# The low part of a filter network's last weights, on 128 stacked rows instead of 64

## The chip, the cores and the metric

The kernel runs on one core of one Trainium2 chip. The time is device time in microseconds, from the first to the last instruction of the program. TensorE is called PE in the profile, its weight loads PEld, VectorE is DVE, ScalarE is ACT, GpSimd is POOL and SyncE, which issues most DMAs, is SP.

## What is computed

One inference step of a two-layer backbone, for a prompt of 128 positions and a sample of 512. Each layer normalises its input, multiplies it with `w_in`, runs three mixers side by side (retention, Hyena, a gated linear recurrence), and multiplies the result with `w_out`. The Hyena mixer convolves along the sequence with long filters, and these filters come from a small network over the position. That network is what the change touches:

```python
hid = jnp.sin(fr[0] * (z @ w1 + b1))            # z (L, 33), w1 (33, 64)
hid = jnp.sin(fr[1] * (hid @ w2 + b2))          # (L, 64)
h = (hid @ w3).reshape(L, 2, 2, 512)            # w3 (64, 2048)
h = h * jnp.exp(-t * deltas)[:, None, None, :]
h = h / (jnp.sum(jnp.abs(h), axis=0, keepdims=True) + EPS)
```

It runs for both lengths, L = 128 and L = 512, in each of the two layers; the kernel keeps both lengths side by side, 640 columns.

## The kernel before

**Split products.** The operands of large products are kept in two parts, a high part in a rounded format (`fp32r`) and a low part, the rest. A product is then the sum of high x high, high x low and low x high.

**The last layer of the filter network.** The 64 hidden values of a position are stacked on 128 partitions: rows 0 to 63 of `hstk` hold the high part, rows 64 to 127 the low part. `w3` (64 rows) is loaded twice, on partitions 0 to 63 and on 64 to 127 (`load_w3`, L598). One product of `w3h`, the high part of the weights on all 128 rows, with `hstk` gives high x high + high x low. `w3l`, the low part of the weights, lies on 64 partitions and is multiplied with the upper 64 rows of `hstk`, which gives low x high. Both go to the same PSUM tile.

**Taps, in `filters` (L594).** Each layer's filters are made in four units `u` of two halves `t`. For one (u, t), `taps(u, t)` converts 256 columns of weights (ACT at L619, DVE at L620), then does four pairs of products (L630 and L631: two directions d by two halves n of 320 columns), each pair into a PSUM tile `hg`. DVE multiplies each tile with a window into SBUF (L632), ACT sums absolute values (L634), and DVE scales and combines (L636 to L647). Later the taps are transposed on PE (`turn`, tiles `ft` and `ftp`), folded (`fold`, L507, on DVE and POOL), split into parts (`blocks`, L534) and transformed by a DFT as products with constant matrices (`dft`, tiles `spr`, `spi`, `spa`).

**Order.** PE runs its instructions in the order in which they are emitted. Threads are generators that emit one stage and yield an estimated time; `pump` chooses the next ready one. A product counts its columns for this clock:

```python
n = x.free_size()
return queue(T.matmul(out, lhs, x, start=start, stop=stop), w * n / 2400 * (4 if x.dtype == F32 else 1))
```

The filters of layer 0 run as a thread among the norm, the modulation (`ada_gen`, tiles `ada`, weights `aw`) and the input projection of layer 0 (tiles `z`, `mtile_steps`). The filters of layer 1 run among the output projection of layer 0 (tiles `o`, `out_proj`) and the modulation of layer 1. The small PSUM tiles (`pat`) share four buffers in turn: `ft`, `ftp`, `hg`, `spr`, `spi`, `spa` and others take the next one, and wait until its last reader is done. The projections use two larger buffers of their own (`pmt`).

Of the kernel before, what the change touches and what calls it, by code (L numbers as in the profile page):

```python
# [16 lines left out]
P = 128  # L17
# [189 lines left out]
# which engine, and at which step: bit masks and step numbers  # L207
# [5 lines left out]
# lead times of the threads, in units of TensorE work  # L213
# [9 lines left out]
def step_kernel(ctx: ExitStack, tc: tile.TileContext, xT, ada_w, w_in, w_out, vecs, fw1, fw2, fw3, lgw, sret,  # L223
# [16 lines left out]
    def f(ap):  # L240
        return ap.bitcast(F32)
# [4 lines left out]
    hstk, w3h, w3l = R1[:, 0:640], R1[:, 640:896], R1[0:64, 896:1152]  # L246
# [61 lines left out]
    # ---------------------------------------------------------------- order of the work on TensorE  # L308
    # TensorE runs its instructions in the order of emission. Threads are generators that emit one
    # stage and yield the time (us of TensorE work) until the next one's operands are there.  # L310
# [49 lines left out]
    def gap(us):  # L360
        """other threads' work while the operands of the next instruction come."""
        end = clk[0] + us
        pump()
        while clk[0] < end:
            clk[0] = min([end] + [max(t.ready, clk[0]) for t in ths])
            pump()
# [9 lines left out]
    # ---------------------------------------------------------------- setup  # L376
# [10 lines left out]
    # decay rates: softplus(-x) of the LRU lambdas and the retention logits  # L387
# [6 lines left out]
    def decays():  # L394
        x, sp = ar(spx_, 32), ar(sp_, 32)
        E = G if XG else V
        for l in range(DEPTH):
            E.tensor_copy(ar(spx_ + 16 * l, 8), vec(l, "lam", 0, 8))
            E.tensor_copy(ar(spx_ + 16 * l + 8, 8), vec(l, "rl", 0, 8))
        a, n, y, q = ar(tA_, 32), ar(tB_, 32), ar(tC_, 32), ar(tD_, 32)  # L400

        def fma(out, u, c, w, op0, op1):
            """(u op0 c) op1 w"""
            if XG:
                G.tensor_scalar(out, u, c, None, op0=op0)
                G.tensor_tensor(out, out, w, op=op1)
            else:
                V.scalar_tensor_tensor(out, u, c, w, op0=op0, op1=op1)

        V.scalar_tensor_tensor(a, x, -1.0, x, op0=ALU.mult, op1=ALU.max)  # L410
        E.tensor_scalar(a, a, 85.0, None, op0=ALU.min)
        E.tensor_scalar(n, a, 1.0 / math.log(2.0), MAGIC, op0=ALU.mult, op1=ALU.add)
        E.tensor_scalar(n, n, MAGIC, None, op0=ALU.subtract)
        fma(y, n, LN2_1, a, ALU.mult, ALU.subtract)
        fma(q, n, LN2_2, y, ALU.mult, ALU.add)
        E.tensor_copy(y, q)
        # 2^-n by its exponent
        E.tensor_scalar(a.bitcast(mybir.dt.int32), n, -float(2 ** 23), 127.0 * 2 ** 23, op0=ALU.mult, op1=ALU.add)
        E.tensor_scalar(q, y, 1.0 / 5040, None, op0=ALU.mult)
        for c in (720, 120, 24, 6, 2, 1):  # L420
            fma(q, q, 1.0 / c, y, ALU.add, ALU.mult)
        fma(q, q, 1.0, a, ALU.add, ALU.mult)
        E.tensor_scalar(a, q, 2.0, None, op0=ALU.add)
        V.reciprocal(a, a)
        E.tensor_tensor(a, a, q, op=ALU.mult)
        E.tensor_tensor(y, a, a, op=ALU.mult)
        E.tensor_scalar(q, y, 1.0 / 15, None, op0=ALU.mult)
        for c in (13, 11, 9, 7, 5, 3):
            fma(q, q, 1.0 / c, y, ALU.add, ALU.mult)
        fma(q, q, 1.0, a, ALU.add, ALU.mult)  # L430
        E.tensor_scalar(a, x, -1.0, 0.0, op0=ALU.mult, op1=ALU.max)
        fma(sp, q, 2.0, a, ALU.mult, ALU.add)
        E.tensor_scalar(ar(sp2_, 32), sp, 2.0, None, op0=ALU.mult)
        E.tensor_scalar(ar(spm4_, 32), sp, -4.0, None, op0=ALU.mult)
        # retention columns: half rate and minus rate
        for l in range(DEPTH):
            E.tensor_scalar(ar(sp2_ + 16 * l + 8, 8), ar(sp_ + 16 * l + 8, 8), 0.5, None, op0=ALU.mult)
            E.tensor_scalar(ar(spm4_ + 16 * l + 8, 8), ar(sp_ + 16 * l + 8, 8), -1.0, None, op0=ALU.mult)
        for i in range(DEPTH):
            E.tensor_scalar(ar(hgb_[i], 16), vec(i, "lgb", 0, 16), 0.5, None, op0=ALU.mult)  # L440

    # ---------------------------------------------------------------- adaLN
# [10 lines left out]
    def ada_gen(l, r, early=False):  # L453
        """Third r of the modulation of layer l; two weight slots per yield."""
# [41 lines left out]
    # ---------------------------------------------------------------- hyena filters  # L496
# [10 lines left out]
    def fold(src, off, eng):  # L507
        """src [P, 4, 256] time blocks -> the eight folded blocks: four at off, four in place."""
        f = ar(off, 1024).rearrange("p (b c) -> p b c", b=4)
        eng.tensor_tensor(f[:, 0:2], src[:, 0:2], src[:, 2:4], op=ALU.add)  # L510
        eng.tensor_tensor(f[:, 2:4], src[:, 0:2], src[:, 2:4], op=ALU.subtract)
        V.scalar_tensor_tensor(src[:, 1], f[:, 3], SQH, src[:, 0], op0=ALU.mult, op1=ALU.add)
        V.scalar_tensor_tensor(src[:, 3], f[:, 1], SQH, src[:, 2], op0=ALU.mult, op1=ALU.add)
        V.scalar_tensor_tensor(src[:, 0], f[:, 3], -SQH, src[:, 0], op0=ALU.mult, op1=ALU.add)
        V.scalar_tensor_tensor(src[:, 2], f[:, 1], SQH, src[:, 2], op0=ALU.mult, op1=ALU.subtract)
        V.tensor_tensor(f[:, 0], f[:, 0], f[:, 1], op=ALU.add)
        V.scalar_tensor_tensor(f[:, 1], f[:, 1], -2.0, f[:, 0], op0=ALU.mult, op1=ALU.add)
        return f[:, 0:2], f[:, 2:4], src[:, 1:4:2], src[:, 0:3:2]
# [4 lines left out]
    def cf0(ri, i):  # L523
        """class 0: half the columns for block i, zeros for the other block's"""
        return cf(192 * ri + 64 * i)

    def mm3(out, w, x, first=True, last=True):
        """out += w.T x of operands split in two parts."""
# [5 lines left out]
    def blocks(fo, pr, cls, eng):  # L534
        """the one or two folded blocks of class cls (E0, prompt, E2, O1, O3), split: [(high, low), ...]"""
# [9 lines left out]
    def dft(out, bl, cls, ri):  # L545
        """part ri of class cls of its blocks."""
# [16 lines left out]
    def hidden(l):  # L563
        """the hidden layers of the layer's filter network, split and stacked."""
# [29 lines left out]
    def filters(l):  # L594
        """Spectra of the layer's filters, to DRAM; yields between pieces of work."""
# [16 lines left out]
        def taps(u, t):  # L612
# [7 lines left out]
            V.tensor_tensor(w3l.rearrange("p (d c) -> p d c", d=2), w3[0:64], f(w3h[0:64]).rearrange("p (d c) -> p d c", d=2),  # L620
# [3 lines left out]
            for d in range(2):  # L624
                h = ar(ROPE_ if d and t else fb_ + 640 * d, 640)
                fd.append(h)
                for n in range(2):
# [3 lines left out]
                    mm(out, w3l[:, 128 * d:128 * d + 128], hs[0:64], start=False, stop=True)  # L631
# [21 lines left out]
        def turn(u, i, t):  # L653
            """part i (sum, difference) of taps t of unit u, time-major."""
# [14 lines left out]
        def hook(u, c):  # L669
            """what goes with class step c (sums 0 to 4, differences 5 to 9) of unit u"""  # L670
# [64 lines left out]
    # ---------------------------------------------------------------- norm  # L735
# [5 lines left out]
    def sumsq(acc, k, hf=None):  # L741
        """squares of X_k: added to acc, but for the last ones (taken by halves), which stay in their buffer."""
# [10 lines left out]
    def rstd(nm, n, *srcs):  # L753
        """1/rms of n columns of summed squares, on all partitions."""
# [15 lines left out]
    def make_h0():  # L770
        """h of layer 0 from the normalised x."""
# [29 lines left out]
    def make_h(l, hf, ks, rs):  # L801
        """columns of half hf of h's tiles ks, from x and 1/rms"""
# [18 lines left out]
    # ---------------------------------------------------------------- projections  # L821
# [16 lines left out]
    def mtile_steps(ps, h, lo, ns):  # L838
        """h @ w of one tile into the halves ns, four products per step."""
# [28 lines left out]
    def both(l, *mts):  # L868
        """two tiles side by side, while the operands come one by one"""
# [15 lines left out]
    def first_half(l, mt):  # L885
        """the half 0 of a tile, before the other's operands are there"""
# [17 lines left out]
    def to_time(src, nm):  # L904
        """five transposes of a channel-major [P, 644]: the sample's four blocks and the prompt's."""
# [6 lines left out]
    # ---------------------------------------------------------------- hyena  # L912
# [164 lines left out]
    def conv_consts():  # L1077
        """the inverse transform's matrices, split: high at 2048, low at 4096 and (the prompt's) in hstk."""
# [10 lines left out]
    # ---------------------------------------------------------------- retention  # L1089
# [4 lines left out]
    def ret_tables(l, early):  # L1094
        """decay tables; the early ones go to DRAM until their place is free."""
# [76 lines left out]
    def ret_in(l, h, start):  # L1172
        """q, k and v of a head"""
# [83 lines left out]
    # ---------------------------------------------------------------- RG-LRU  # L1257
# [11 lines left out]
    def lru_pad_init(l):  # L1269
        """per (ct, dir) the four pad columns of the scan input: zero, and the initial state next to the sample."""  # L1270
# [78 lines left out]
    # ---------------------------------------------------------------- gates, output projection  # L1349
# [104 lines left out]
    # ---------------------------------------------------------------- schedule  # L1454
# [243 lines left out]
```

## Time and profile before

| | |
|---|---|
| median of 3 runs | 1324.87 us (1324.29 to 1326.26) |
| span of the profiled execution | 1326.2 us |
| PE busy | 1184.6 us, 89% |
| PE weight loads busy | 1104.7 us, 83% |
| DVE busy | 910.2 us, 69% |
| ACT busy | 619.0 us, 47% |
| POOL busy | 629.9 us, 48% |
| instructions | 20592 |
| mean granted clock of PE | 0.954 |

Busy time is the time in which an engine has an instruction under way. A wait is shown with what ended it: the engine, the tile and the line whose result came last; "issue" stands for a wait that nothing in the profile explains. The end of a matmul is modelled, so the starts of weight loads and matmuls tell more than the durations. The granted clock is 1.00 at 2.4 GHz and 0.50 at 1.2 GHz.

### The profile page before, as it was taken

How to read it: one execution, taken by the hardware profiler on the slowest of the kernel's cores; microseconds unless marked ns; L12 is line 12 of the kernel's file. 1: busy time of each engine (PE TensorE's matmuls, PEld its weight loads, DVE VectorE, ACT ScalarE, POOL GpSimd, SP SyncE). 2: the span in 40 equal slices, each digit the busy share in tenths (PEclk: the TensorE clock that was granted, in tenths of full speed). 3: DMA queues.
4: the chain of work that ended last, by engine and by line, in shares of the span. 5: the costliest groups of instructions: out<-in, count | busy, mean ns of one | idle time of the engine just before them, and what ended most of it. 6: DMA issues, size and time to landing. Idle time of an engine off the chain costs nothing. (4 is left out here: it accounts for less than half of the span.)

```text
span 1326.2 us, 20592 instructions
## 1 busy us (share of the span) xinstructions
PE 1184.6 (89%) x7944; PEld 1104.7 (83%) x7944; DVE 910.2 (69%) x1412; ACT 619.0 (47%) x1099; POOL 629.9 (48%) x529
## 2 busy tenths in 40 slices
PE   4688899998989889869999988899999989889996
PEld 2476779997989889857777778899998989888996
DVE  6888886685865777666887669665477576676313
ACT  3557555343334566644455554432443366555220
POOL 2644436554555644442334438454354654545431
PEclk9798899999999899988999989899999998999998
DMA  9632323312211112244454623122221211124222
GB/s 331 212 126 90 120 87 111 130 62 72 88 39 62 56 48 65 90 130 134 151 165 154 213 70 114 50 102 80 73 88 41 68 48 64 34 69 122 69 63 80
DMA packets 52114, 131.62 MB, mean 99 GB/s; under 512 B 6230, under 2 KB 14182, under 8 KB 50736
## 3 DMA queue, kind: packets, MB, share of 16 engines
q1 hardware_dynamic: 51668, 130.21, 29.5%
q8 instruction: 62, 1.02, 0.3%
q14 instruction: 36, 0.29, 0.1%
q10 hardware_dynamic: 348, 0.11, 0.0%
HBM read 112.38 MB, written 17.92 MB: 98 GB/s over the span
## 5 line engine op out<-in xcount | busy, mean ns | idle before, releaser
L296 ACT ACTIVATE r<-arena 128x512 fp32r<-128x512 f32 (+1 forms) x72 | 43.6, 607 | 113.8 <-PE u L328 37.7
L296 ACT ACTIVATE arena<-arena 128x644 f32<-128x644 f32 (+5 forms) x84 | 63.5, 772 | 46.3 <-DVE arena L1392 33.8
L296 ACT ACTIVATE rt<-arena 128x512 fp32r<-128x512 f32 (+1 forms) x42 | 29.1, 692 | 98.9 <-POOL arena L980 78.8
L328 PE MATMUL u<-r,cfwd 128*128 128x256 f32 x432 | 63.2, 295 | 12.4 <-ACT r L296 9.6
L328 PEld LDWEIGHTS u<-r,cfwd 128*128 128x128 f32 x432 | 58.4, 201 | 14.5 <-ACT r L296 10.8
L328 PE MATMUL hg<-r 128*128 128x320 f32 (+1 forms) x128 | 48.6, 441 | 18.9 <-DVE r L589 9.5
L542 POOL TENSOR_TENSOR r<-arena,r 128x512 fp32r<-128x512 f32 (+1 forms) x24 | 31.7, 1322 | 68.1 <-ACT r L296 58.0
L1392 DVE SCALAR_TENSOR_TENSOR arena<-o,arena 128x128 f32<-128x128 f32 (+2 forms) x48 | 18.5, 432 | 60.2 <-PE o L328 60.1
L328 PEld LDWEIGHTS hg<-r 128*128 128x128 f32 (+1 forms) x128 | 25.7, 201 | 40.9 <-issue 18.7
L980 POOL TENSOR_TENSOR arena<-arena 128x256 f32<-128x256 f32 x40 | 39.2, 980 | 34.4 <-DVE arena L976 17.7
L975 DVE TENSOR_TENSOR arena<-u,arena 128x512 f32<-128x512 f32 x40 | 27.5, 688 | 31.7 <-PE u L328 31.7
L296 ACT ACTIVATE arena<-z 128x644 f32<-128x644 f32 x44 | 31.0, 705 | 35.9 <-PE z L328 35.8
L328 PE MATMUL spr<-r,cfwd 128*128 128x256 f32 x192 | 36.8, 303 | 10.6 <-ACT rt L296 4.0
L328 PEld LDWEIGHTS spr<-r,cfwd 128*128 128x128 f32 x192 | 29.0, 198 | 17.2 <-ACT rt L296 5.5
L983 POOL TENSOR_TENSOR rt<-arena,rt 128x512 fp32r<-128x512 f32 x24 | 31.9, 1331 | 20.0 <-ACT rt L296 20.0
L542 DVE TENSOR_TENSOR r<-arena,r 128x512 fp32r<-128x512 f32 x32 | 34.2, 1067 | 9.6 <-ACT r L296 8.6
L296 ACT ACTIVATE r<-rt 128x512 fp32r<-128x512 f32 (+3 forms) x50 | 28.2, 564 | 21.0 <-PE spi L328 7.7
L328 PE MATMUL spi<-r,cfwd 128*128 128x256 f32 x168 | 35.7, 301 | 0.9 <-DVE rt L632 0.9
L542 POOL TENSOR_TENSOR r<-rt,r 128x256 fp32r<-128x256 f32 (+1 forms) x16 | 19.2, 1199 | 36.4 <-ACT r L296 36.3
L296 ACT ACT_TABLE_LOAD x27 | 34.6, 1283 | 3.8 <-DMA arena<-in_vecs 3.3
L542 POOL TENSOR_TENSOR dm<-rt,r 128x256 fp32r<-128x256 f32 (+1 forms) x16 | 21.6, 1347 | 28.6 <-ACT r L296 28.6
L1334 DVE TENSOR_TENSOR_SCAN lr<-arena 128x644 f32<-128x644 f32 x8 | 18.4, 2294 | 24.1 <-POOL arena L1329 24.1
(1285 smaller groups left out, 4279.2 us busy)
## 6 DMA issues: line engine op xcount, KB each, us to landing
w<-in_w_in SPq DMA_DIRECT2D x80, 512.0 KB
aw<-in_ada_w SPq DMA_DIRECT2D x96, 256.0 KB
wo<-in_w_out SPq DMA_DIRECT2D x32, 384.0 KB
spec<-arena SPq DMA_DIRECT2D x16, 640.0 KB
arena<-spec SPq DMA_DIRECT2D x8, 1280.0 KB
arena<-in_xT SPq DMA_DIRECT2D x16, 320.0 KB
rt<-in_c_win SPq DMA_DIRECT2D x4, 640.0 KB
arena<-xspill SPq DMA_DIRECT2D x8, 320.0 KB
```

Of the source, the lines that this page charges most:

```text
L296: return S.activation(out, in_, f, bias=bias, scale=scale)
L328: return queue(T.matmul(out, lhs, x, start=start, stop=stop), w * n / 2400 * (4 if x.dtype == F32 else 1))
L542: eng.tensor_tensor(lo, src, f(h), op=ALU.subtract)
L975: V.tensor_tensor(y, pv, hre[:, c].unsqueeze(1).broadcast_to([P, 2, 256]), op=ALU.mult)
L980: G.tensor_tensor(y[:, 1], y[:, 1], m2[:, 0], op=ALU.add)
L983: (G if PY >> c & 1 else V).tensor_tensor(lo, yo, f(h), op=ALU.subtract)
L1334: V.tensor_tensor_scan(hout, m, b, 0.0, op0=ALU.mult, op1=ALU.add)
L1392: V.scalar_tensor_tensor(x, ps[:, pc:pc + n], ar(mod_[l] + 32 + 2 * mt + s, 1), x, op0=ALU.mult, op1=ALU.add)
```

## The change

`w3l` gets all 128 partitions of its 256 columns of `R1`. DVE's subtraction at L620 fills both halves, and the second product of each pair takes all 128 rows of `hstk`, so it adds low x high + low x low. Number and order of the instructions stay as they are. In the rest of the diff only comments are taken out.

```diff
-    hstk, w3h, w3l = R1[:, 0:640], R1[:, 640:896], R1[0:64, 896:1152]
+    hstk, w3h, w3l = R1[:, 0:640], R1[:, 640:896], R1[:, 896:1152]
...
             act(w3h.rearrange("p (d c) -> p d c", d=2), w3)
-            V.tensor_tensor(w3l.rearrange("p (d c) -> p d c", d=2), w3[0:64], f(w3h[0:64]).rearrange("p (d c) -> p d c", d=2),
+            V.tensor_tensor(w3l.rearrange("p (d c) -> p d c", d=2), w3, f(w3h).rearrange("p (d c) -> p d c", d=2),
                             op=ALU.subtract)
...
                     mm(out, w3h[:, 128 * d:128 * d + 128], hs, start=True, stop=False)
-                    mm(out, w3l[:, 128 * d:128 * d + 128], hs[0:64], start=False, stop=True)
+                    mm(out, w3l[:, 128 * d:128 * d + 128], hs, start=False, stop=True)
                     V.tensor_tensor(h[:, 320 * n:320 * n + 320], out, ar(win + 640 * t + 320 * n, 320), op=ALU.mult)
```

## Rows read from the trace of the kernel before

**Rows 1.** The page, part 1: busy us, share of the span, instructions.

```profile
PE 1184.6 (89%) x7944; PEld 1104.7 (83%) x7944; DVE 910.2 (69%) x1412; ACT 619.0 (47%) x1099; POOL 629.9 (48%) x529
```

**Rows 2.** Groups by form, PE, whole span: shapes, count, busy us, mean ns, idle.

```profile
L328 PE MATMUL hg<-r 64*128 64x320 f32 x64 | 28.5, 445 | 0.0
L328 PE MATMUL hg<-r 128*128 128x320 f32 x64 | 27.9, 436 | 18.9 <-DVE r L589 9.5 <-ACT r L296 8.6 <-ACT rt L296 0.6
...
L328 PE MATMUL z<-hl,w_17h 128*128 128x322 f32 x32 | 8.4, 310 | 0.0
```

**Rows 3.** Tile hg: its weight loads (ns min/median/max); who waited (us, times).

```profile
L328 PEld LDWEIGHTS hg<-r x128: 182/186/289, 19.9 to 722.1; 128*128 128x128 f32 x64, 64*128 64x128 f32 x64
...
  PEld spr L328: 5.1, 6
```

**Rows 4.** Timeline, PEld, block 12: start us, us, instruction, idle before it.

```profile
647.78 0.22 PEld L328 LDWEIGHTS hg<-r 128*128 128x128 f32 x1
648.16 0.18 PEld L328 LDWEIGHTS hg<-r 64*128 64x128 f32 x1 [0.16 <-issue]
...
650.54 0.19 PEld L328 LDWEIGHTS spi<-r,cfwd 128*128 128x128 f32 x1 [0.16 <-DVE arena L632]
```

**Rows 5.** Timeline, PEld, the input projection at full clock.

```profile
75.08 0.34 PEld L328 LDWEIGHTS z<-hl,w_17h 128*128 128x128 f32 x2
75.37 0.34 PEld L328 LDWEIGHTS z<-hh,w_17h 128*128 128x128 f32 x2
```

**Rows 6.** Timeline, PEld, at half clock: the input projection and block 9.

```profile
63.67 0.60 PEld L328 LDWEIGHTS z<-hl,w_16h 128*128 128x128 f32 x2
64.21 0.60 PEld L328 LDWEIGHTS z<-hh,w_16h 128*128 128x128 f32 x2
...
595.15 0.29 PEld L328 LDWEIGHTS hg<-r 128*128 128x128 f32 x1 [8.84 <-ACT r L296]
...
599.66 0.50 PEld L328 LDWEIGHTS o<-yh,wo000h 128*128 128x128 f32 x2 [0.28 <-issue]
```

**Rows 7.** Timeline, DVE, block 12: first and last evacuation, next weights.

```profile
648.61 0.49 DVE L632 TENSOR_TENSOR rt<-hg,rt 128x320 f32<-128x320 f32 x1 [0.64 <-PE hg L328]
...
650.65 0.49 DVE L632 TENSOR_TENSOR arena<-hg,rt 128x320 f32<-128x320 f32 x1 [0.19 <-PE hg L328]
651.06 0.41 DVE L620 TENSOR_TENSOR r<-w,r 64x256 fp32r<-64x256 f32 x1
```

**Rows 8.** Timeline, DVE and PEld, block 3: evacuations and next PE work.

```profile
82.34 1.68 DVE L632 TENSOR_TENSOR rt<-hg,rt 128x320 f32<-128x320 f32 x4
...
82.87 0.30 PEld L328 LDWEIGHTS spr<-r,cfwd 128*128 128x128 f32 x2 [1.19 <-DVE rt L632]
```

**Rows 9.** Timeline, PEld: the transposes of block 12's taps.

```profile
659.38 0.42 PEld L331 LDWEIGHTS ft<-arena,rt 128*128 128x128 f32 x4 [1.51 <-DVE rt L647]
```

**Rows 10.** Windows: length; busy us of PE, PEld, DVE, ACT, POOL; clock; DMA.

```profile
94.90:98.40 3.50, 3.50 (x17) 2.20 (x18) 1.53 (x5) 1.86 (x5) 0.77 (x1) 0.51 0.02 7
...
600.10:603.50 3.40, 3.40 (x17) 2.26 (x17) 0.55 (x3) 1.96 (x6) 0.32 (x1) 0.50 0.24 77
```

**Rows 11.** Timeline, DVE and PE, after block 1.

```profile
24.50 0.49 DVE L632 TENSOR_TENSOR rt<-hg,rt 128x320 f32<-128x320 f32 x1 [0.63 <-PE hg L328]
24.91 0.82 DVE L1488 TENSOR_TENSOR arena<-arena 128x640 f32<-128x640 f32 x1
...
25.78 0.37 PE L328 MATMUL n<-arena 128*128 128x1 f32 x1 [1.31 <-DVE arena L1488]
```

**Rows 12.** Timeline, DVE, block 2: the last evacuation and the modulation.

```profile
41.45 0.49 DVE L632 TENSOR_TENSOR arena<-hg,rt 128x320 f32<-128x320 f32 x1 [0.59 <-PE hg L328]
...
48.09 0.16 DVE L489 TENSOR_TENSOR arena<-ada,arena 128x16 f32<-128x16 f32 x1
```

**Rows 13.** Timeline, DVE and PEld, block 4: first evacuation and next PE work.

```profile
93.55 0.48 DVE L632 TENSOR_TENSOR rt<-hg,rt 128x320 f32<-128x320 f32 x1
...
95.24 0.29 PEld L328 LDWEIGHTS spi<-r,cfwd 128*128 128x128 f32 x1 [0.27 <-DVE rt L632]
```

## The prediction

> **What bounds the kernel now.** I read part 1 of the page first: PE is busy 89% of the span, DVE 69%, so TensorE is the first suspect [rows 1]. A busy PE is modelled, though, so I went on to the groups of PE and then to its weight loads in order of time, where the starts are what was measured. The reader is to see a contradiction: the two products of the filter network's last layer, on 64 and on 128 rows, last about as long as each other, 445 and 436 ns, but far above the 310 ns of a projection product of nearly the same width [rows 2]. They also follow each other much more slowly. There are 128 of them, from 19.9 to 722.1 us [rows 3]: 16 blocks of eight, high part and low part in turn, eight blocks for each layer's filters. I number them 1 to 16 in time; 1 to 8 run in the input projection of layer 0, 9 to 16 in its output projection.
>
> In block 12 the eight take 2.76 us to the next instruction, 0.345 each, and the weight load stands idle 0.16 before most of them with no releaser but "issue" [rows 4]. The projection's products, all on 128 rows, also change weights each time, yet two take 0.29 us, 0.147 each, with no idle time between [rows 5]. At the lower clock it is the same: 4.51 us for block 9, 0.564 each, against 0.54 for two, 0.27 each [rows 6]. Something stops the weights of the next product from loading under the running one, and it stands wherever 64 and 128 rows alternate. No other difference between the pair and its neighbours shows in these rows.
>
> **The change, part by part.**
>
> *What it adds.* L620 subtracts on 128 partitions instead of 64. It takes 0.41 us for 256 columns on 64 partitions; L632, on 128, takes 0.49 for 320 [rows 7]. That is 1.60 and 1.53 ns a column: DVE time goes by columns. Cost of 16 such: 0. The low product reads rows 64 to 127 of hstk and of the weights too; the high product and the conversion just before them read those already, so no wait is new. No DMA or engine assignment changes, and the planner counts columns alone, so the order of emission stays.
>
> *What it removes.* Of the pairs 64/128 none is left. A new block should run at the pitch of the neighbours: 8 x 0.147 = 1.18 us instead of 2.76 at full clock, 1.58 less; 8 x 0.27 = 2.16 instead of 4.51 at half clock, 2.35 less. Bounds for the pitch: 0.345 (nothing happens) and 0.147; I take 0.147, because the only other thing in which the two rows differ is two columns of 322. Were it all to arrive at the end, 14 x 1.58 + 2 x 2.35 = 26.8 us. It will not, since DVE has to empty each block's four PSUM tiles, and what follows waits for it.
>
> Here a rule of the Trainium skill speaks against the change: "TensorE: Matmul & The Clock Gate", section "LDWEIGHTS (loading the stationary operand)", says that a load's time depends on its columns, not its rows, and the durations agree, 182 to 186 ns from the shortest to the median over both forms [rows 3]. By that rule alone the change is worth 0 and the time stays 1324.87. The same skill, "TensorEngine Tiling (Array Packing)", section "Key Properties", says that a change of tiling mode drains the engine; by that rule the pitch is the price of the changes and the sum is the one below. The rows on pitch decide for the second.
>
> *Where DVE sets the next step: nothing.* In block 3 the evacuations come at 82.34, as DVE is busy with other work, four in 1.68 us, 0.40 apart. The next PE work needs the first one's PSUM buffer and waits 1.19 us [rows 8]. PE done 1.5 us sooner waits that much longer. Blocks 5, 6, 7, 11 and 13 look alike; in all, six spr weight loads wait 5.1 us after blocks [rows 3]. Six blocks: 0 (0 to 1.58 each at most).
>
> *Where PE sets it: 10, 12, 14, 15, 16.* In block 12 each evacuation waits 0.19 for PE, and the first starts 0.45 after the second load [rows 4, 7]. After the change the second load comes at 647.95, the first evacuation from 648.40 to 648.89, and PE is through at 648.96: the next work starts 1.58 earlier. The fourth evacuation ends at 648.40 + 1.68 = 650.08 instead of 651.14, only 1.06 earlier. The transposes of these taps wait at 659.38 for L647, the end of the chain that begins with these evacuations, by 1.51 us [rows 9]; there 0.52 of the 1.58 is given back. So 12 gives 1.06; 14 and 16, whose transposes are about as tight, I count the same. 10 and 15 meet no such wait: 1.58 each. Sum 3 x 1.06 + 2 x 1.58 = 6.3 (5.3 to 7.9).
>
> *Block 9* ends 2.35 earlier, and the output projection behind it is PE's alone. But the granted clock is 0.50, the 1.2 GHz level, up to 603.5 [rows 10]. If it rises at the same moment, the work pulled forward runs at half speed and half is lost: 1.2. If it rises earlier with the denser work, all 2.35 stays. I take 1.8.
>
> *Layer 0.* After block 1 the norm's matmul waits 1.31 for L1488, which DVE runs behind the fourth evacuation; that waited 0.63 for PE [rows 11]. From the first evacuation on, DVE's own work to that point is four of 0.49 and two additions of 0.82, 3.6 us. The first can begin at about 20.8: the block's start at 19.9, 0.27 for the second load and, an estimate from block 12's 0.45, some 0.65 at half clock. That ends at 24.4 instead of 25.7: 1.3 (0 to 2.35). In block 2 the fourth evacuation waits 0.59 for PE, and behind it in DVE's queue stands the tap chain, then L489, which all of layer 0's input waits for [rows 12]: 0.6 (0 to 1.5). After block 4 spi starts at 95.24, though its buffer was free at 94.03 [rows 13]; PE may come 1.1 earlier, but the other evacuations are held by DVE: 0.5 (0 to 1.1). Block 8 alike: 0.5. Sum 2.9.
>
> Total 6.3 + 1.8 + 2.9 = 11.0; by the ends 6.5 (5.3 + 1.2 + 0) to 16.3 (7.9 + 2.35 + 6.05). The profiled execution spans 1326.2, 1.3 above the median of the three runs, so it would be 1315.2, and the median 1313.9. After the last block nothing is anchored: later waits are for work that itself follows PE.
>
> **Rivals.**
>
> *DVE or ACT swallows more.* L647 style waits, or ACT's conversions, may set more of the starts than I count; DVE is at 69% over all and must be fuller than that where PE waits for it. Then only the part that shortens its own chains remains: 2.7 to 6.5 saved, about 1320. For it: six of sixteen blocks already do so. Against: five blocks where DVE stands waiting for PE. Chance 0.18.
>
> *Nearly all comes through,* as earlier PE work also starts DVE's folds earlier, and denser PE work holds the clock: 16.3 to 26.8 saved, 1298 to 1308.6. Against it are the waits for L632. Chance 0.09.
>
> *The change does not do what it says:* the pitch stays 0.345, because the gap belongs to something else in the pair. Time 1324.9. Against it: neighbours on 128 rows, with weights changed each time, run without it. Chance 0.08.
>
> *Slower, by the clock.* Six blocks get more idle PE time behind them, since PE is done before DVE. After block 4, with its slow pitch, the granted clock was 0.51 from 94.9 to 98.4 [rows 10]; such a stretch does half of 3.5 us less work, 1.75. If each of the six brought one, 10.5 of the 11.0 would be gone; it needs eight new stretches, 14.0, to be slower by 2.65. Against it: total PE work in those stretches is as before, and blocks 4 and 8 get denser. Chance 0.07.
>
> **How the numbers follow.** Forecast 1313.9 with chance 0.58. A measurement here can tell about 0.2%, 2.65 us. Faster by more: 0.58 + 0.18 + 0.09 = 0.85; within it 0.08; slower 0.07. The range reaches past the sum's ends to most of the swallowing rival and a little into the better one and one clock stretch either way: 1305.5 to 1322.
>
> **What would show it.** Right: hg products only on 128 rows, at a pitch near 0.15 and near 0.27 at half clock, with no "issue" gaps; blocks of 1.2 us where PE sets the pace; evacuations 0.40 apart in block 12; in blocks 3, 5, 6, 7, 11, 13 the wait for L632 longer by about 1.5; layer 0's L489 about 2 us earlier; the blocks of layer 1 earlier still. Wrong if the pitch stays, if the "issue" gap is found between equal rows too, if waits for L647 grow by as much as the blocks shrink, or if the granted clock falls after the blocks oftener than before.

## The result, and the profile after

The changed kernel takes 1310.18 us (median of 4 runs, 1308.28 to 1312.01), the kernel before in the same comparison 1325.57 us (4 runs, 1324.29 to 1330.52). The ratio is 0.9875, with an interval of 0.9855 to 0.9895: 16.6 us faster by the ratio, between 13.9 and 19.2; the two medians lie 15.4 apart. The forecast was 11.0 us, a time of 1313.9; the range, 1305.5 to 1322, holds the measured time. The same kernel was timed a second time, beside the experiments, and was 12.6 us faster there (8.8 to 16.4). One execution of a later kernel, the one with only the blocks that DVE paces changed, took 2779.19 us where its other eleven took 1322.86 to 1332.44, and its ratio leaves that one out.

The changed kernel does as many products as before, with PE, ACT and POOL in the same order; DVE's instructions differ only in the shape of L620. Part 1 of the page after, beside [rows 1]:

```profile
PE 1156.0 (88%) x7944; PEld 1097.5 (84%) x7944; DVE 907.0 (69%) x1412; ACT 618.0 (47%) x1099; POOL 631.4 (48%) x529
```

PE is busy 28.6 us less, and the weight loads only 7.2: what went is time between a load and the product that follows, not time in loads. The groups of PE by form show where, beside [rows 2]:

```profile
L328 PE MATMUL hg<-r 128*128 128x320 f32 x128 | 26.5, 345 | 20.1 <-DVE r L589 9.5 <-ACT r L296 8.5 <-ACT rt L296 1.1
...
L328 PE MATMUL z<-hl,w_17h 128*128 128x322 f32 x32 | 8.5, 310 | 0.0
```

The two groups of 64, 445 and 436 ns each, have become one of 128 at 345, and the neighbour on 128 rows stays at 310. Together they are busy 26.5 us, before 28.5 + 27.9 = 56.4. So 29.9 us of busy time left the products of the filter network, and about half of that came through to the end. The tile's view tells where some of the rest went, beside [rows 3]:

```profile
L328 PEld LDWEIGHTS hg<-r x128: 186/188/333, 20.3 to 706.9; 128*128 128x128 f32 x128
...
  PEld spr L328: 11.8, 5
...
  PEld spi L328: 1.4, 2
```

The weight loads of `spr` now wait 11.8 us behind the blocks, before 5.1. In order of time the weight loads of blocks 1, 3, 9 and 12, and the transposes of block 12's taps, are these (the timeline of PEld, as in [rows 4, 6, 8, 9, 11]):

```profile
20.29 2.10 PEld L328 LDWEIGHTS hg<-r 128*128 128x128 f32 x8 [10.58 <-DVE r L589]
24.57 0.71 PEld L328 LDWEIGHTS n<-arena 128*128 128x128 f32 x3 [2.18 <-DVE arena L1488]
...
77.15 1.17 PEld L328 LDWEIGHTS hg<-r 128*128 128x128 f32 x8 [0.41 <-issue]
80.93 0.53 PEld L328 LDWEIGHTS spr<-r,cfwd 128*128 128x128 f32 x4 [2.61 <-DVE rt L632]
...
587.67 0.29 PEld L328 LDWEIGHTS hg<-r 128*128 128x128 f32 x1 [8.77 <-ACT r L296]
588.13 1.83 PEld L328 LDWEIGHTS hg<-r 128*128 128x128 f32 x7 [0.17 <-DVE r L620]
589.90 0.60 PEld L328 LDWEIGHTS o<-yh,wo000h 128*128 128x128 f32 x2
...
636.48 1.23 PEld L328 LDWEIGHTS hg<-r 128*128 128x128 f32 x8
637.67 0.19 PEld L328 LDWEIGHTS spi<-r,cfwd 128*128 128x128 f32 x1
...
646.56 0.42 PEld L331 LDWEIGHTS ft<-arena,rt 128*128 128x128 f32 x4 [1.49 <-DVE rt L647]
```

The reader is to see three kinds of block. Block 12 takes 637.67 - 636.48 = 1.19 us where it took 2.76; its eight loads are one row of the view now, since no idle time parts them. Block 9, at half clock, takes 2.23 where it took 4.51. Block 3 is as quick as block 12, but what follows it waits 2.61 for DVE's L632 instead of 1.19, so 1.42 of its gain is gone at once. DVE's side, with its own timeline (as [rows 7, 8, 12]):

```profile
46.14 0.16 DVE L489 TENSOR_TENSOR arena<-ada,arena 128x16 f32<-128x16 f32 x1
...
80.39 1.68 DVE L632 TENSOR_TENSOR rt<-hg,rt 128x320 f32<-128x320 f32 x4
...
637.11 0.89 DVE L632 TENSOR_TENSOR rt<-hg,rt 128x320 f32<-128x320 f32 x2 [0.45 <-PE hg L328]
637.92 0.88 DVE L632 TENSOR_TENSOR arena<-hg,rt 128x320 f32<-128x320 f32 x2
638.71 0.42 DVE L620 TENSOR_TENSOR r<-w,r 128x256 fp32r<-128x256 f32 x1
```

In block 12 DVE has taken over as the one that sets the pace: the four evacuations follow each other without idle time. L620 on 128 partitions takes 0.42 us, on 64 it took 0.41.

Since PE's order is the same in both kernels, the start of the same weight load can be compared all along the program. This table is worked out from the timelines of PEld (start after less start before, us), for both profiles of the changed kernel and for two experiments that are told of below; the last column adds up the prediction's terms.

| load, and its start before | after | second profile of after | blocks 1, 2, 4, 8 only | blocks 4, 8 only | forecast |
|---|---|---|---|---|---|
| input projection of layer 0 under way, 50.98 | -1.95 | -2.20 | -2.40 | -0.10 | -1.9 |
| behind block 4, 103.82 | -4.14 | -4.21 | -4.61 | -2.29 | -2.4 |
| before block 8, 178.05 | -4.79 | -4.94 | -5.19 | -2.76 | -2.4 |
| behind block 8, 184.32 | -6.92 | -7.06 | -7.33 | -4.88 | -2.9 |
| before block 9, 582.81 | -7.54 | -5.06 | -5.70 | -3.88 | -2.9 |
| behind block 9, 601.17 | -9.66 | -6.96 | -5.64 | -3.58 | -4.7 |
| layer 1, 1005.48 | -15.51 | -15.40 | -6.03 | -4.29 | -11.0 |
| last load, 1318.65 | -18.05 | -18.05 | -8.55 | -6.91 | -11.0 |

One profile is one execution, and its half-clock stretches lie elsewhere in the next. Four kernels that are told of below have blocks 1, 2, 4 and 8 as before (DVE's part alone, blocks paced by DVE, layer 1 alone, block 6 alone); on the same rows down to 582.81 they shift by -1.35 to +2.30. So a step of one or two microseconds in a single column is not proof of a block's gain.

The last step of 2.5 us is in all four columns alike, and in the three other profiles of kernels that gained. In the three that gained nothing it is absent: they shift from +1.0, +2.4 and +2.0 at 1005.48 to +1.7, +3.0 and +2.8 at the end. Its first 1.5 us come at a half-clock stretch of the kernel before; the windows start at the same load, before and after (length; busy us of PE, PEld, DVE, ACT, POOL; clock; DMA):

```profile
1016.50:1020.00 3.50, 3.50 (x18) 3.50 (x17) 1.61 (x3) 0.28 (x1) 3.32 (x4) 0.51 0.26 75
1001.00:1004.50 3.50, 3.50 (x28) 3.50 (x27) 2.85 (x5) 1.05 (x3) 3.34 (x4) 1.00 0.31 74
```

From that load on the clock is 0.57 to 0.58 in the three without gain and 1.00 in the seven with one. No block lies near, so whether this step comes with the change or with the executions that were profiled is open. Without it 15.5 are left in the profile. From before block 9 on the two profiles of the changed kernel gain 8.0 and 10.3 where 8.1 was forecast; up to there they gain 7.5 and 5.1 where it was 2.9. So it is layer 0 that has to be explained.

### The profile page after: what moved, and what is told of

Read it like the earlier page. It is cut to its first block, busy times and chain, and to the rows that moved or that the text cites. A ratio compares the mean times of both kernels' runs of the same rounds, so it can differ in the third digit from the quotient of the medians.

```text
span 1308.1 us, 20591 instructions
## 1 busy us (share of the span) xinstructions
PE 1156.0 (88%) x7944; PEld 1097.5 (84%) x7944; DVE 907.0 (69%) x1412; ACT 618.0 (47%) x1099; POOL 631.4 (48%) x529
## 5 line engine op out<-in xcount | busy, mean ns | idle before, releaser
L328 PE MATMUL spr<-r,cfwd 128*128 128x256 f32 x192 | 37.0, 304 | 16.5 <-DVE rt L632 10.5
L328 PEld LDWEIGHTS spr<-r,cfwd 128*128 128x128 f32 x192 | 29.2, 198 | 22.8 <-DVE rt L632 11.8
L328 PE MATMUL hg<-r 128*128 128x320 f32 x128 | 26.5, 345 | 20.1 <-DVE r L589 9.5
L328 PEld LDWEIGHTS hg<-r 128*128 128x128 f32 x128 | 21.0, 206 | 24.4 <-DVE r L589 10.6
```

## Experiments

All are made from the changed kernel, each run beside the kernel before on one chip; on the chips of these comparisons that one took 1326.7 to 1329.5 us, so the ratios are what counts.

**DVE's part alone.** L620 stays on 128 partitions, and the low product takes the upper 64 rows again.

```diff
-                    mm(out, w3l[:, 128 * d:128 * d + 128], hs, start=False, stop=True)
+                    mm(out, w3l[0:64, 128 * d:128 * d + 128], hs[0:64], start=False, stop=True)
```

> DVE subtracts on 128 partitions as in the changed kernel, but the low product takes 64 rows again. Theory A (the cost is the alternation of 64 and 128 rows on TensorE): pitch in a block back at 0.345 us, block 12 back at 2.76, time within 2.6 us of the kernel before, 1323 to 1328. Theory B (part of the gain came from the subtraction or from the shift of DVE's work): below 1320. Theory C (the 64-row product is slow by itself): the same as A here.

1326.1 us, ratio 0.9988 (0.9972 to 1.0004): nothing. The weight loads of block 12 stand as in [rows 4], 0.34 apart with 0.15 to 0.16 of "issue" between:

```profile
647.71 0.19 PEld L328 LDWEIGHTS hg<-r 128*128 128x128 f32 x1 [0.16 <-issue]
648.05 0.18 PEld L328 LDWEIGHTS hg<-r 64*128 64x128 f32 x1 [0.16 <-issue]
```

So none of the gain comes from DVE's part; it needs the product on 128 rows.

**Fewer changes, but still 64 rows.** The second pair of each direction is issued with the low product first, so that a block runs high, low, low, high, high, low, low, high: as many products on 64 rows as before, and half the changes.

```diff
-                    mm(out, w3h[:, 128 * d:128 * d + 128], hs, start=True, stop=False)
-                    mm(out, w3l[:, 128 * d:128 * d + 128], hs, start=False, stop=True)
+                    for i, (w_, k) in enumerate(((w3h, P), (w3l, 64))[::1 - 2 * n]):
+                        mm(out, w_[0:k, 128 * d:128 * d + 128], hs[0:k], start=i == 0, stop=i == 1)
```

> Low product on 64 rows, but every second pair is issued low part first, so that a block runs high, low, low, high, high, low, low, high: 4 changes of row count instead of 8, and as many 64-row products as before. Theory A: about 0.2 us per change, so block 12 takes 8 x 0.147 + 4 x 0.2 = 1.97 us, products behind an equal row count follow at 0.147 with no issue gap, and about half of the 15.4 us is gained: 1315 to 1320. Theory C: every 64-row product still stops the load behind it and before it, block 12 stays near 2.7, time 1323 to 1328.

1318.04 us, ratio 0.9936 (0.9908 to 0.9963), 8.5 us faster (4.9 to 12.2), about half of what the change gives. The timeline of PEld, block 12:

```profile
641.40 0.22 PEld L328 LDWEIGHTS hg<-r 128*128 128x128 f32 x1
641.77 0.29 PEld L328 LDWEIGHTS hg<-r 64*128 64x128 f32 x2 [0.15 <-issue]
642.26 0.30 PEld L328 LDWEIGHTS hg<-r 128*128 128x128 f32 x2 [0.19 <-issue]
642.75 0.29 PEld L328 LDWEIGHTS hg<-r 64*128 64x128 f32 x2 [0.19 <-issue]
643.23 0.19 PEld L328 LDWEIGHTS hg<-r 128*128 128x128 f32 x1 [0.19 <-issue]
643.34 0.19 PEld L328 LDWEIGHTS spi<-r,cfwd 128*128 128x128 f32 x1
```

Two loads of the same row count merge into one row of the view, 64 rows as well as 128; the idle time stands only where the count changes. The block takes 1.94 us. Eight at 0.147 and four changes at 0.345 - 0.147 = 0.198 are 1.97. So it is the change of row count that costs, not the 64 rows.

**Blocks that DVE paces, alone.** 128 rows in blocks 3, 5, 7, 11 and 13 only. The diff, as those below, is written with a name `k` for the row count.

```diff
-                    mm(out, w3l[:, 128 * d:128 * d + 128], hs, start=False, stop=True)
+                    k = P if (l, u, t) in ((0, 1, 0), (0, 2, 0), (0, 3, 0), (1, 1, 0), (1, 2, 0)) else 64
+                    mm(out, w3l[0:k, 128 * d:128 * d + 128], hs[0:k], start=False, stop=True)
```

> 128 rows only in blocks 3, 5, 7, 11 and 13, where VectorE's evacuations set the next work; 64 rows in the other eleven. Theory A with the terms of the prediction: TensorE waits longer for L632 and nothing is gained, 1323 to 1328. Rival D (all TensorE time counts, by way of earlier chains or the clock): 5 x 1.58 = 7.9 gained, about 1318.

1328.43 us, ratio 0.9994 (0.9973 to 1.0014): nothing, though five blocks are 1.5 us shorter each. Who waits for tile `hg` (us, times):

```profile
  PEld spr L328: 11.9, 6
```

The waits, 5.1 us before [rows 3], have grown by 6.8, which is what the five blocks gave, less 0.7.

**One layer at a time.** The row count is 128 in layer 1 alone (`k = P if l else 64`), and in another kernel in layer 0 alone (`k = 64 if l else P`).

> 128 rows only in layer 1's blocks 9 to 16. By the shifts read from the traces of before and after, from -7.2 at the start of the output projection to -15.4 behind block 16, this half gives 8.2 and with the drift behind it up to 10: 1316 to 1318. By the prediction's terms 6.3 + 1.8 = 8.1: 1317.5. Rival E (the order of VectorE's and GpSimd's work in layer 0 is what gained most): less than 6 here, above 1319.5.

> 128 rows only in layer 0's blocks 1 to 8. By the shifts read from the traces of before and after (-5.5 to -7.5 between block 8 and the output projection): 6 to 7.5 gained, ratio 0.9943 to 0.9955. By the prediction's terms for layer 0: 2.9, ratio 0.998. If the surplus of layer 0 was chance (where the clock fell, which of VectorE and GpSimd began first), it may be near the second.

Layer 1 alone: 1320.94 us, ratio 0.9947 (0.9923 to 0.9970), 7.0 us faster (4.0 to 10.2); forecast 8.1. Layer 0 alone: 1320.45 us, ratio 0.9936 (0.9917 to 0.9955), 8.5 us faster (6.0 to 11.0); forecast 2.9. The term for layer 1 stands; that for layer 0 is outside its interval.

**The changed kernel again.**

> The changed kernel again, on the same chip as the three others: ratio 0.9855 to 0.9895, as first measured.

1317.97 us, ratio 0.9905 (0.9877 to 0.9934), 12.6 us faster (8.8 to 16.4). The forecast of 11.0 lies inside this interval and below the first one's. The six executions spread from 1309.88 to 1320.49 us.

**Taps later, so that DVE has time.** The three places at which a unit's taps are made among its class steps are moved back by one.

```diff
-PT0, PT1, PT2 = 2, 5, 8
+PT0, PT1, PT2 = 3, 6, 9
```

> The changed kernel with a layer's taps issued one class step later (steps 3, 6 and 9 instead of 2, 5 and 8), so that VectorE has its fold behind it when the evacuations come. If the waits for L632 behind blocks 3, 5, 7, 11 and 13 (11.8 us in the changed kernel) are what is left of the gain, some 4 to 8 us less than the changed kernel, ratio to the kernel before about 0.983. Rival: the wait only moves to the transposes, which wait for L647, and nothing is gained: 0.9875, or worse.

1337.95 us, ratio 1.0058 (1.0037 to 1.0080): slower than the kernel before. The waits of PE after the move, the longest two (us in total, times, longest):

```profile
PE spr L328 <- ACT r L296: 15.8, 6, 4.8
PE ft L331 <- DVE rt L647: 13.8, 8, 2.6
```

L632 no longer stands at the top of this list, where the changed kernel has it with 10.5 us; `spr` waits for ACT's conversions instead, 15.8 us, and the transposes wait for L647 13.8 us instead of 8.4. The order chosen for the old pitch is not improved by a step of one.

**The same idea at the modulation.** The modulation's products use 32 columns, and beside them the loads stand idle too. Two k steps were issued together, to halve the changes between 32 and 128 columns; that takes four weight slots at a time instead of two.

```diff
-            w = [slot(f"aw{l}{r}{k}{j}")[:, 0:512] for j in range(2)]
...
+            if early or k % 2 == 0:
+                w = [slot(f"aw{l}{r}{k}{j}")[:, 0:512] for j in range(2 if early else 4)]
...
-                yield LA if k else LA0 if l == 0 else LA02
+                yield 2 * LA if k else LA0 if l == 0 else LA02
```

> The changed kernel, with the modulation's products (32 columns of the array each) of two k steps issued together in the three thirds per layer that run among other work, so that TensorE changes between 32 and 128 columns 16 times less each way, and VectorE adds 16 times less. Theory A extended to columns: each visit loses about 0.4 to 0.6 us at its ends, 16 x 0.4 = 6.4 us of TensorE time, of which two thirds reach the end as for the rows: ratio to the kernel before about 0.984. Rival: the gaps of 0.41 us are hidden or belong to the products themselves: 0.9875, or worse by later weights.

1361.68 us, ratio 1.0252 (1.0227 to 1.0276). The longest wait of PE:

```profile
PE ada L328 <- DMA aw<-in_ada_w: 30.5, 10, 5.0
```

The weights come too late, and whatever halving the changes may give is buried under 30.5 us of waiting for them. What these changes cost stays open.

**Layer 0, the four blocks that were counted.** 128 rows in blocks 1, 2, 4 and 8 only. Here the first theory of the surplus was tested, that block 6 had stopped waiting for DVE.

```diff
+                    k = P if (l, u, t) in ((0, 0, 0), (0, 0, 1), (0, 1, 1), (0, 3, 1)) else 64
```

> The low product has 128 rows only in blocks 1, 2, 4 and 8, the four of layer 0 that the forecast counted with 2.9 us together; in the twelve others it keeps 64. With 128 rows in all eight blocks of layer 0 the median fell by 8.5 us (6.0 to 11.0). Theory A (the four counted terms were too small, and what follows them comes along: the clock stays full after block 4, and block 6, which keeps its slow pitch here, is still less held by DVE because all before it comes sooner): 5 to 8 us faster. Theory B (the forecast's sizes hold for these four, and the surplus comes from block 6 having 128 rows itself): 2 to 4 us faster, and the start of the transposes after block 6 no earlier than 3 us before the kernel before.

1319.25 us, ratio 0.9941 (0.9922 to 0.9959), 7.8 us faster (5.4 to 10.4), about as much as all eight blocks. So the surplus goes with these four, as far as the two intervals tell. One half of theory A did not come: L1120 in front of block 6 still takes 3.24 us, and block 6 is held by DVE as before.

**Block 6 alone** (`k = P if (l, u, t) == (0, 2, 1) else 64`).

> The low product has 128 rows only in block 6. Theory A (block 6 gains only where the work before it comes sooner, so that DVE's tap product L1120 runs ahead of POOL's split L828): L1120 is still as long as 3.3 us and just ahead of the evacuations, the wait for L632 grows by about 1.5 us, and the time stays within 1 us of the kernel before. Theory B (the forecast was wrong to set block 6 at nothing, since 128 rows there are worth their 1.58 us even alone): 1 to 2.5 us faster, and the wait for L632 after block 6 as in the kernel before or shorter.

1327.92 us, ratio 0.9992 (0.9975 to 1.0008). The timeline of PEld:

```profile
136.04 0.60 PEld L328 LDWEIGHTS hg<-r 128*128 128x128 f32 x4 [0.42 <-ACT rt L296]
138.77 0.29 PEld L328 LDWEIGHTS spi<-r,cfwd 128*128 128x128 f32 x1 [2.13 <-DVE rt L632]
```

The wait for L632 was 1.14 and is 2.13. Nothing comes through, as forecast for block 6.

**Blocks 4 and 8 alone.** The forecast's sum has no term for the granted clock behind these two blocks. Here is a window of 3.5 us behind block 4 and one behind block 8, in two kernels. First the kernel with only block 6 changed, where blocks 4 and 8 have the slow pitch (length; busy us of PE, PEld, DVE, ACT, POOL; clock; DMA):

```profile
94.90:98.40 3.50, 3.50 (x17) 2.17 (x17) 1.25 (x4) 1.65 (x4) 0.53 (x1) 0.50 0.02 7
180.60:184.10 3.50, 3.50 (x14) 3.22 (x14) 0.51 (x2) 1.58 (x6) 0.50 (x1) 0.50 0.03 8
```

Over ten profiles, of all kernels so far but the two that move taps or modulation, the split is clean. Blocks 4 and 8 have the slow pitch in five (before, DVE's part alone, blocks paced by DVE, layer 1 alone, block 6 alone): 0.50 to 0.56 behind them, near the 1.2 GHz level. In the other five, the kernel with half the changes among them, and in the one below, the clock is 1.00 behind both. The next kernel has 128 rows in these two blocks and nowhere else.

```diff
+                    k = P if (l, u, t) in ((0, 1, 1), (0, 3, 1)) else 64
```

> The low product has 128 rows only in blocks 4 and 8; in the other fourteen it keeps 64. In the 3.5 us that follow the last load of these two blocks the granted clock was 0.50 to 0.56 in all profiles in which they ran at the slow pitch, and 1.00 in all in which they did not. Theory A (the forecast left out that the denser blocks keep the clock at its upper level behind them, worth up to 1.7 us of work each on top of the 0.5): clock 1.00 behind both blocks here too, TensorE's work some 2 us earlier behind each, and the median 2.5 to 5 us below the kernel before. Theory B (the forecast's 0.5 each holds, and the clock behind blocks 4 and 8 is a matter of what blocks 1 and 2 shift): clock 0.5 behind at least one of them, TensorE's work 1 us earlier in all, time within 2 us of the kernel before.

1321.54 us, ratio 0.9960 (0.9942 to 0.9977), 5.3 us faster (3.1 to 7.7). The same windows:

```profile
93.30:96.80 3.50, 3.04 (x25) 2.16 (x24) 3.50 (x8) 2.15 (x7) 1.10 (x1) 1.00 0.47 142
176.40:179.90 3.50, 2.90 (x21) 2.64 (x21) 2.16 (x5) 2.01 (x6) 0.71 (x1) 1.00 0.40 150
```

PE does 25 products in the first window instead of 17, and even stands idle for 0.46 us. Two blocks that the forecast put at 0.5 each bring 2.2 and 2.1 us (the table's fifth column: from -0.10 to -2.29, from -2.76 to -4.88), of which 0.8 behind block 4 and 0.4 behind block 8 are lost again at the next waits. The blocks themselves and the clock have about equal parts in it: at the load that follows the block (95.24, 181.20 in the kernel before) 1.15 and 1.03 are there, and the other 1.05 and 1.09 come in the next 3 us, which the kernel before spends at half clock. Theory A holds, with some 1.1 for the clock where it allowed up to 1.7.

## Why the forecast was right, and where it was too small

*The price of a change of row count: right.* The pitch is 1.19 / 8 = 0.149 in block 12 (forecast 0.147) and 0.268 at half clock in block 9, from 588.30 to 589.64, the starts of the third and the last load, five steps (forecast 0.27). The kernel with half the changes shows that the price belongs to the change and not to the 64 rows: 0.198 us each at full clock; at half clock it is 0.564 less 0.268, about 0.30. The Trainium skill, "TensorEngine Tiling (Array Packing)", section "Key Properties", says that a change of tiling mode drains the engine; the runs agree in that each change costs and an equal count beside it does not, but no row shows the draining itself. By the rule of the Trainium skill, "TensorE: Matmul & The Clock Gate", section "LDWEIGHTS (loading the stationary operand)", that a load's time goes by columns alone, nothing should have been gained. It holds for the loads themselves, 182 to 188 ns from the shortest to the median at either row count, but their time isn't what this change saves.

*DVE-paced blocks at nothing: right.* Blocks 3, 5, 7, 11 and 13 alone give nothing, and block 6 alone gives nothing. Block 7 does not look like the others, though: before, nothing waited behind it, its next load came 0.34 after its last one; with 128 rows that load comes 1.73 after, so the time turned into a wait all the same. In the changed kernel block 6 is not held by DVE, for a reason told in the last section; in its second profile it is, and the total is the same.

*Blocks 10, 12, 14, 15 and 16 at 6.3, block 9 at 1.8: right in sum, in part by luck.* Layer 1 gains 8.0 and 10.3 in the two profiles and 7.0 (4.0 to 10.2) alone, with 8.1 forecast. In block 12 the last evacuation was to end 2.30 us after the block's start; it ends at 638.79, 2.31 after. The transposes of these taps were to wait 0.52 longer for L647; they wait 1.49 where it was 1.51, so that part of the working erred by half a microsecond, on the safe side. Block 10 errs the other way. It was to meet no wait; from its first load to the next work it takes 1.75 us where it took 2.73, 0.98 less and not 1.58, since its fifth load now waits 0.60 for ACT:

```profile
599.34 0.59 PEld L328 LDWEIGHTS hg<-r 128*128 128x128 f32 x4
600.53 0.59 PEld L328 LDWEIGHTS hg<-r 128*128 128x128 f32 x4 [0.60 <-ACT rt L296]
```

Blocks 14 and 16 wait for ACT too, 0.46 and 0.26, and shrink by 1.09 and 1.33. What block 12 gave beyond its term, 0.5, and what block 10 fell short, 0.6, cancel in the sum. Block 9 gains 2.1 and 1.9: most of it stays.

*Blocks 1 and 2 at 1.9: right as far as the profiles tell.* L489 comes at 46.14 instead of 48.09, 1.95 sooner. The four profiles with 128 rows in these blocks shift by -1.65 to -2.40 at the first row of the table, five with 64 rows there by -0.10 to -1.35.

*Blocks 4 and 8 at 0.5 each: the term that was mis-sized.* They measure 2.2 and 2.1, and 1.4 and 1.7 after the next waits. The working priced the edit by when DVE lets go of the PSUM buffer, at full clock, and let the clock behind block 4 [rows 10] serve only as a price for the rival "slower, by the clock". It was a term with the other sign: the half-clock stretch stood behind the slow pitch, and it went with it. With only these two blocks changed that was 1.05 and 1.09, less than the rival's 1.75, since TensorE now stands idle for part of the time (0.46 us behind block 4). The blocks themselves gave 1.15 and 1.03 at the next load, the upper end of the range of 0 to 1.1, of which the next waits took 0.8 and 0.4 back.

This does not make up the whole surplus. Some 1.9 for blocks 1 and 2 and 1.4 and 1.7 for blocks 4 and 8 are 5.0 of the 8.5 (6.0 to 11.0) that layer 0 gives alone. The first profile has 1.4 more between blocks 4 and 8 (from -3.3 at 114.4 to -4.8 at 178.05), but DVE's part alone shifts by as much between these rows (from +0.3 to -1.1), with every product as before, so this need not be the dense products' doing. The step of 2.5 behind 1005.48 is in the profile of layer 0 alone too. Where the rest comes from stays open.

*The rivals.* That nearly all comes through falls in its strong form, since 11.8 us of waits for L632 stand behind the blocks; but its second half, denser work that holds the clock, is a part of what made the forecast too small. That DVE swallows more, and that the change doesn't do what it says, fall with the result. The new idle stretches behind blocks 3, 5, 7, 11 and 13 did not lower the clock over all, 0.954 in both profiled executions.

*What stays open.* The two comparisons of the changed kernel differ, 16.6 and 12.6 us, with intervals that overlap from 13.9 to 16.4. Within one kernel the time goes with the granted clock of the execution. In the second comparison the changed kernel took 1319.26 to 1320.49 us in its three executions at a mean clock of 0.944 to 0.947, and 1309.88 to 1316.67 in the three at 0.953 to 0.958; all four of the first comparison lie at 0.954 to 0.960. The kernel before took 1329.28 to 1330.85 in its three at 0.945 to 0.946, so at a like clock the change is worth some 10 us there. What sets an execution's clock the runs don't tell. Where the half-clock stretches fall shows in the table as well. Between blocks 8 and 9, where no block lies, the first profile of the changed kernel gains 0.6 more and the second gives back 2.0: at the loads that the kernel before runs from 378.2 to 381.7 the clock is 0.51 there, 0.52 in the second profile and 1.00 in the first.

## What to carry to other kernels

Products whose row counts alternate between 64 and 128 pay about 0.2 us at every change on these rows; filling the missing rows, even with work that the result does not need, or ordering equal counts side by side, takes it away, and the place to see it is the idle time of the weight loads, not the products' durations. Before summing the gain, find for each stretch who empties PSUM: where that engine sets the pace, the time turns into a wait of the same size. And where a slow-pitched stretch is followed by work at the lower clock, count that work too: here it was worth about as much as the stretch itself. Before a step of one or two microseconds in a profile is put down to an edit, look whether a kernel without that edit shows it too.

## What was not expected of the hardware

**The clock behind a busy but slow stretch.** In the kernel before PE counts as busy for 3.00 of 3.00 us around block 4 at the slow pitch (92.5 to 95.5), and the clock falls behind it; with the dense pitch PE is idle for part of the windows behind blocks 4 and 8, and the clock stays at 1.00. Busy time on the page said nothing of it; the pitch did. A fall can still come later: in both profiles of the changed kernel the clock is 0.51 from 192.3 to 195.7, where the kernel before has 1.00 at the same loads, and some 1.4 us of the lead is lost there; with only blocks 4 and 8 changed it is not.

**One DVE instruction at its own time or well over twice that, by 0.2 us of order.** L1120 on DVE and L828 on POOL start together in front of block 6. In the kernel before (timelines of POOL and DVE):

```profile
135.21 2.36 POOL L828 TENSOR_TENSOR w_25l<-w,w_25h 128x1024 fp32r<-128x1024 f32 x1
...
135.35 3.31 DVE L1120 SCALAR_TENSOR_TENSOR arena<-arena 128x1032 f32<-128x1032 f32 x1
...
140.98 1.22 DVE L1121 SCALAR_TENSOR_TENSOR arena<-arena 128x1032 f32<-128x1032 f32 x1
```

In the changed kernel's first profile:

```profile
130.82 1.66 DVE L1120 SCALAR_TENSOR_TENSOR arena<-arena 128x1032 f32<-128x1032 f32 x1
...
131.90 2.84 POOL L828 TENSOR_TENSOR w_25l<-w,w_25h 128x1024 fp32r<-128x1024 f32 x1 [0.51 <-PE z L328]
```

With only blocks 4 and 8 changed (DVE, then POOL):

```profile
133.89 1.22 DVE L1120 SCALAR_TENSOR_TENSOR arena<-arena 128x1032 f32<-128x1032 f32 x1
134.02 3.32 POOL L828 TENSOR_TENSOR w_25l<-w,w_25h 128x1024 fp32r<-128x1024 f32 x1 [0.41 <-DVE arena L477]
```

Where POOL starts first, by 0.14 to 0.22 us, DVE takes 3.24 to 3.31 us (five profiles) and POOL 2.36 to 2.39. Where DVE starts first by 0.13, it takes 1.22 and POOL 3.32; where it starts 1.07 to 1.08 ahead, it takes 1.65 to 1.66 and POOL 2.81 to 2.85 (four profiles). The like instruction L1121 takes 1.22. The Trainium skill, "SBUF — State Buffer", section "SBUF: two separate sides", says that a DVE instruction with two SBUF inputs and a GpSimd instruction that reads SBUF exclude each other for a whole instruction, and the one that starts first goes first. These rows agree in order of size: 3.31 is near the 2.22 us that L828 still runs plus 1.22, and 3.32 near the 1.09 that L1120 still runs plus 2.36. The 1.66 where DVE is a full 1.08 ahead doesn't follow from it. Which of the two starts first is not set by the dense products: in layer 1 alone, with layer 0's products as before, DVE is first, and in DVE's part alone POOL is. No experiment turned the order round on purpose.
